# Two layers of a hybrid encoder: four old states to a tile, products of half and quarter width issued side by side

## The chip, the cores and the metric

The kernel runs on one core of one Trainium2 chip. The metric is the device time of one execution in microseconds (us), from the first to the last instruction of the core. PE is the tensor engine (PEld its weight loads), DVE the vector engine, ACT the scalar engine, POOL the GpSimd engine, SP the queue that issues every transfer of this kernel.

## What is computed

A prompt of 256 positions and 8 samples of 16 positions (384 columns in all) pass two layers of width 1024 that share all weights. Each layer has three mixers side by side (windowed attention, a state-space scan, a gated mixing of positions), their projections and gates, and a squared-ReLU block of width 4096. Cut to the two mixers that the change touches:

```python
def sink_attend(q, k, v, valid, sinks):          # 8 query heads in 2 groups of 4, one k/v head a group
    s = jnp.einsum('bcqkgd,bcnkd->bckgqn', q, k) * (HEAD_DIM ** -0.5)
    p = jnp.exp(s - m[..., None])
    o = jnp.einsum('bckgqn,bcnkd->bcqkgd', p, v) / denom

def ssd_scan(x, dt, a, bm, cm, h0):              # h0: old state, 16 heads x 64 x 128 for each sample
    chunk_state = jnp.einsum('bcsgn,bcsgk,bcsgkp->bcgkpn', bc, decay_end, xdt)
    h_new = chunk_decay * h0 + chunk_state       # written out for each sample
    y_inter = jnp.einsum('bctgn,bcgkpn->bctgkp', cc, h_in) * jnp.exp(cum)[..., None]
    y = y_intra + y_inter
```

## The kernel before

**Tiling.** Activations lie with features on the 128 partitions and the 384 columns (256 prompt, 128 samples) along the row. A weight unit is 128 x 1024 f32 (512 KB). SP loads it into one of 4 `raw` tiles (L159), ACT rounds it to a high half (`whi`, L141), DVE subtracts for the low half (`wlo`, L142), 4 tiles of each, and PE multiplies high by high, low by high and high by low, 24 products of 384 columns a unit. These ordinary products fill most of PE's time.

**Order of the work.** The mixers' small products are written as a generator, `chores` (L927): the loops over the weight units call `side()` (L965) before each unit, and a step of the chores is issued there, so that small work lies between ordinary products. A planner then lays the program out over the engines with its own costs; each engine, and SP's queue, runs its instructions in that order. The chores are, layer by layer: turning k and q, `scores` (L651), `turn_p` (L668), `values` (L679) and `attended` (L684) for the prompt, `attn_sample` (L689) for the samples, and `ssd(0)`, `ssd(1)` (L782) for the two groups of state-space heads.

**Scores and values.** The two k/v heads lie on partitions 0 to 63 and 64 to 127. `scores` multiplies all products of one head, then those of the other (64 rows of the array each, into two PSUM banks). `values` writes one head's output to 64 partitions of the bank `po`, so that a product uses 64 columns of the array; it is issued for one head as soon as that head's probabilities are turned, and for the other a step later. For the samples each head has one product of 512 columns and eight of 64.

**Old states.** In `ssd(g)` each of the 8 samples has an old state of 128 x 512 (half the heads). `state` (L895) loads it into a tile of the pool `tm` (12 tiles of 128 x 512). `sample` (L883) multiplies it by 32 columns of `cpad` (L886): C of this sample, with zeros in its neighbour's place, so a product uses 32 columns of the array and all 128 rows, and its 32 partitions of the bank `py` take the sum of two samples. Then PE makes the update from the stacked factors (L890, `stack` and `bm`), POOL scales the old state into a second tile `hn` (L891), DVE adds (L892) and SP writes the result (L893). One sample is one step of the chores:

```python
hn = tm()
mm(py[r, :], cpad[:, b % 2, r], hb, b % 2 == 0, b % 2 == 1)
...
mm(p, bm[:96], d[:96, 0:512], True, True)
pool.tensor_tensor(heads(hn), heads(hb), hb_(decb[:, b, hs]), ALU.mult)
dve.tensor_tensor(hn, hn, p, ALU.add)
```

Beside it run the products within chunks: `decay` (L847, half on POOL, half on DVE, L851) makes the factors of `mask` (L855), and `within` (L864) uses the mask a step later. An f32 product of PE has two records in the trace, a rounded one (`whi`, `wlo`, `stack`, `s1r`) one record.

Of the kernel before, what the change touches and what calls it, by code (L numbers as in the profile page):

```python
# [61 lines left out]
def trunk_kernel(ctx, tc, x_in, c_in, w_ada, sm_in, gf_in, cn_in, wst, wkv, gmc, kc_in, vc_in, hs_in, cs_in,  # L62
# [8 lines left out]
    def nm(s):  # L71
        ids[0] += 1
        return f"{s}{ids[0]}"
# [16 lines left out]
    def mm(out, lhsT, rhs, start, stop):  # L90
        pe.matmul(out, lhsT, rhs, start=start, stop=stop, skip_group_check=True)  # L91
# [53 lines left out]
    class Stream:  # L145
        """The weights of a layer, by group; now and then a part of the modulation's."""
# [66 lines left out]
    def ada(blocks, raws=raw_tile, bank=acc):  # L213
        """Two blocks of the first layer's modulation in three steps: loads, products, the rest."""
# [22 lines left out]
    def ada4(pb):  # L237
        """The rest of the modulation, four blocks at a time; two units of the weights in each step."""
# [41 lines left out]
    class Norm:  # L280
        """1 / sqrt(mean of squares over the features), for each token, in all partitions."""
# [66 lines left out]
    class Early:  # L348
        """The products x * scale, and the shifts beside them: what a layer's first products take while the norm is computed."""
# [24 lines left out]
    def settle(p, rstd, relu):  # L374
        """Products of Early's columns, with the norm and the shifts."""
# [50 lines left out]
    # the tensor engine's clock is up by the time that its first operands are there  # L426
# [31 lines left out]
    def mixers(l, pa, st, h, first):  # L458
        def tm(dt=F32):
            return pa.tile([128, 512], dt, tag="tm", name=nm("tm"), bufs=12)  # L460
# [15 lines left out]
        # gMLP, doubled up to the product  # L476
# [38 lines left out]
        # k, v, dt  # L515
# [12 lines left out]
        # dt = softplus(raw + bias), log1p(e) = 2 atanh(e / (2 + e))  # L528
# [20 lines left out]
        # sums of dt * a: up to t, after s, all; of each sample, all  # L549
# [4 lines left out]
        # q  # L554
# [7 lines left out]
        # rotary  # L562
# [18 lines left out]
        # sums of dt * a: up to t, after s, all; of each sample, all  # L581
# [32 lines left out]
        # gMLP's mixing of positions  # L614
# [53 lines left out]
        def turn_p(i, ng, es, kh):  # L668
            pts = []
            for kt in range(i + 1):  # L670
# [4 lines left out]
                act.copy(pt[:, :ng * 128], p[:, :ng * 128])  # L675
                pts.append(pt)
            return pts
# [6 lines left out]
        def attended(i, g0, ng, po):  # L684
# [4 lines left out]
        def attn_sample():  # L689
# [27 lines left out]
            po = yi()  # L717
            for kh in range(2):
                w = slice(64 * kh, 64 * kh + 64)
                pts = []  # L720
                for src in (pns[kh], pcs[kh]):
# [4 lines left out]
                    act.copy(pt, p)  # L726
# [14 lines left out]
        # convolution  # L741
# [40 lines left out]
        def ssd(g):  # L782
# [35 lines left out]
            # states of the prompt  # L818
# [17 lines left out]
            def stack(j):  # L836
                """The factors of two samples' updates, one below the other: high by high, low by high, high by low."""
# [8 lines left out]
            # within chunks  # L846
# [48 lines left out]
            def state(b):  # L895
                hb = tm()
                sp.dma_start(out=hb, in_=hs_in[l, :, b, half])
                return hb

            todo = [(0, 0), (1, 0), (0, 1), (1, 1), (0, 2), (1, 2)]  # L900
            hb, rs, m, d = state(0), decay(*todo[0]), None, stack(0)
            yield
            for n in range(8):
                if n < 7:
                    nxt = state(n + 1)
                if n % 2 == 0 and n < 6:
                    ahead = stack(n // 2 + 1)
# [7 lines left out]
                sample(n, hb, d)  # L915
                if n % 2:
                    d = ahead
                hb = nxt
                yield
            yin[2] = tm()  # L920
# [6 lines left out]
        def chores():  # L927
# [13 lines left out]
            pts = [turn_p(0, 4, es, kh)for kh in range(2)]  # L941
            turn_q(2)
            yield
            po = yi()
            for kh in range(2):
                values(0, 4, po, kh, pts[kh])
            attended(0, 0, 4, po)
            for g0 in (0, 2):
                es = scores(1, g0, 2, 256)
                yield  # L950
                po = yi()
                pts = turn_p(1, 2, es, 0)
# [275 lines left out]
```

## Time and profile before

| what | value |
|---|---|
| time, median of 3 runs | 1513.43 us (1512.86 to 1515.37) |
| profiled execution, first to last instruction | 1513.4 us |
| PE busy / its weight loads | 1489.4 us (98%) / 1343.3 us |
| DVE, ACT, POOL busy | 918.2, 639.8, 364.7 us |
| old states: loads and writes | 32 and 32 of 256 KB |
| mean DMA rate | 157 GB/s |

The profiled execution is taken over the same stretch as the times, so its span is its own time, and it stands at the median. Busy time is the union of the records of an engine or a group; a matmul's record runs on while the next one starts, so starts are what tells the pace. Times in a timeline are us from the span's start. Layer 0's mixers run from about 60 to 360 us, layer 1's from about 800 to 1100 us; `ssd(0)` and `ssd(1)` of layer 0 have their samples at 222 to 262 and 292 to 340 us.

### The profile page before, as it was taken

To read this page: it belongs to the slowest core of one execution; us is meant where nothing else is said; L and a number is where in the kernel's file an instruction comes from. 1 tells how busy PE (TensorE), PEld (TensorE's weight loads), DVE (VectorE), ACT (ScalarE), POOL (GpSimd) and SP (SyncE) were. 2 spreads that over 40 slices of the span, in tenths; PEclk is the share of its full clock that TensorE was granted. 3 is DMA by queue.
4 is the path that set the end of the run, shared out by engine and by line. 5 is a ranking of instruction groups with operands and counts; after the bars stand their busy time and mean duration, and the time that the engine had idled before them with its cause. 6 is when DMAs were issued, how large, how long until landed. Compare 5 with 4: busy or idle time off the path is not lost.

```text
span 1513.4 us, 22955 instructions
## 1 busy us (share of the span) xinstructions
PE 1489.4 (98%) x8656; PEld 1343.3 (89%) x8656; DVE 918.2 (61%) x1585; ACT 639.8 (42%) x1142; POOL 364.7 (24%) x553
## 2 busy tenths in 40 slices
PE   8999999999999999999999999999999999999997
PEld 6888887879999988889897988878799999999997
DVE  5688856657456855444448887566674667554332
ACT  4466532325335644322225665423253456443221
POOL 3263223340114500011116623233401254000000
PEclk9999999999999999999999999999999999999999
DMA  9453346454344565565552622363533333333331
GB/s 376 155 196 112 116 151 202 165 190 139 140 167 140 172 237 205 210 221 218 213 186 78 213 95 88 116 197 120 181 123 112 126 112 125 126 126 126 126 126 42
DMA packets 79519, 237.04 MB, mean 157 GB/s; under 512 B 10032, under 2 KB 16560, under 8 KB 79408
## 3 DMA queue, kind: packets, MB, share of 16 engines
q1 hardware_dynamic: 79408, 235.57, 44.9%
q8 instruction: 68, 1.11, 0.3%
q14 instruction: 43, 0.35, 0.1%
HBM read 219.21 MB, written 12.39 MB: 153 GB/s over the span
## 4 chain that ended last, share of the span: by engine, by line
PE 95%; DVE 2%; issue 1%; POOL 1%; ACT 1%; DMA 0%; SPq 0%; DVEq 0%; POOLq 0%; ACTq 0%
PE acc L91 74%; PE mx L91 10%; PE yi L91 6%; PE yy L91 4%; PE mx L129 1%; DVE wlo L142 1%; DMA x<-in_x_dram 0%; DVE x L1090 0%; DVE hlo L345 0%; PE yy L129 0%; PE yi L129 0%; ACT whi L141 0%; POOL h L338 0%; PE acc L129 0%; POOL ck L385 0%
## 5 line engine op out<-in xcount | busy, mean ns | idle before, releaser
L142 DVE TENSOR_TENSOR wlo<-raw,whi 128x1024 fp32r<-128x1024 f32 (+1 forms) x296 | 377.6, 1278 | 261.8 <-ACT whi L141 259.0
L141 ACT CAST whi<-raw 128x1024 fp32r<-128x1024 f32 (+1 forms) x296 | 305.5, 1037 | 511.0 <-PE acc L91 422.9
L91 PE MATMUL acc<-hhi,whi 128*128 128x384 f32 x1264 | 433.9, 343 | 3.7 <-ACT ck L1060 2.2
L91 PE MATMUL acc<-hhi,wlo 128*128 128x384 f32 x1264 | 429.0, 339 | 1.0 <-DVE wlo L142 1.0
L91 PE MATMUL acc<-hlo,whi 128*128 128x384 f32 x1264 | 428.6, 341 | 0.0
L91 PEld LDWEIGHTS acc<-hhi,whi 128*128 128x128 f32 x1264 | 237.3, 188 | 30.1 <-ACT ck L1060 11.7
L91 PEld LDWEIGHTS acc<-hlo,whi 128*128 128x128 f32 x1264 | 237.4, 188 | 9.5 <-issue 8.4
L91 PEld LDWEIGHTS acc<-hhi,wlo 128*128 128x128 f32 x1264 | 237.5, 188 | 6.7 <-issue 4.5
L91 PE MATMUL acc<-fhi,whi 128*128 128x384 f32 x512 | 173.8, 339 | 0.0
L91 PE MATMUL acc<-fhi,wlo 128*128 128x384 f32 x512 | 172.0, 336 | 0.0
L91 PE MATMUL acc<-flo,whi 128*128 128x384 f32 x512 | 172.0, 336 | 0.0
L91 PE MATMUL acc<-quad,whi 128*128 128x384 f32 (+1 forms) x576 | 152.6, 343 | 0.0
L91 PEld LDWEIGHTS acc<-quad,whi 128*128 128x128 f32 x576 | 104.7, 188 | 5.4 <-issue 4.9
L91 PEld LDWEIGHTS acc<-fhi,whi 128*128 128x128 f32 x512 | 96.2, 188 | 12.6 <-issue 11.7
L91 PE MATMUL acc<-quad,wlo 128*128 128x384 f32 (+1 forms) x288 | 97.6, 339 | 0.0
L91 PEld LDWEIGHTS acc<-flo,whi 128*128 128x128 f32 x512 | 96.3, 188 | 0.0
L91 PEld LDWEIGHTS acc<-fhi,wlo 128*128 128x128 f32 x512 | 96.2, 188 | 0.0
L367 POOL TENSOR_TENSOR rs<-x,gains 128x128 f32<-128x128 f32 x24 | 28.2, 1177 | 209.2 <-DVE x L419 209.2
L292 POOL TENSOR_TENSOR ck<-x 128x128 f32<-128x128 f32 x5 | 4.9, 982 | 259.4 <-DVE x L419 252.0
L208 ACT CAST fhi<-ck 128x384 fp32r<-128x384 f32 x64 | 32.4, 512 | 52.9 <-DVE ck L1061 52.9
L91 PEld LDWEIGHTS acc<-quad,wlo 128*128 128x128 f32 x288 | 54.3, 189 | 0.2
L768 DVE SCALAR_TENSOR_TENSOR tm<-tm,cwh,tm 128x408 f32<-128x408 f32 x72 | 47.2, 663 | 4.2 <-ACT tm L766 3.8
(338 smaller groups left out, 2115.8 us busy)
## 6 DMA issues: line engine op xcount, KB each, us to landing
raw<-in_wst_dram SPq DMA_DIRECT2D x288, 512.0 KB, 3.3
raw<-in_w_ada_dram SPq DMA_DIRECT2D x52, 512.0 KB, 4.0
early<-in_w_ada_dram SPq DMA_DIRECT2D x44, 512.0 KB, 5.1
tm<-in_hs_dram SPq DMA_DIRECT2D x32, 256.0 KB, 3.3
out_ss_dram<-tm SPq DMA_DIRECT2D x32, 256.0 KB, 2.6
stack<-tm SPq DMA_DIRECT2D x48, 64.0 KB, 2.5
tm<-in_gmc_dram SPq DMA_DIRECT2D x10, 256.0 KB, 4.3
raw<-in_wkv_dram SPq DMA_DIRECT2D x8, 272.0 KB, 2.6
```

Source lines behind the costliest of these rows:

```text
L91: pe.matmul(out, lhsT, rhs, start=start, stop=stop, skip_group_check=True)
L129: pe.transpose(out, in_, ident[:rows, :rows])
L141: act.copy(hi[:, :n], raw[:, :n])
L142: dve.tensor_tensor(lo[:, :n], raw[:, :n], hi[:, :n].bitcast(F32), ALU.subtract)
L208: act.copy(hi, t)
L292: pool.tensor_tensor(t[:, NP:], ap[:, NP:], ap[:, NP:], ALU.mult)
L367: pool.tensor_tensor(smp(s[:, 0:128]), smp(x[:, k, NP:]), bt(a[:, 1:9]), ALU.mult)
L768: dve.scalar_tensor_tensor(y[:, n], xp[:, i:i + 408], cw[:, c, i:i + 1], y[:, n], ALU.mult, ALU.add)
```

## The change

- **Old states:** `states(q)` loads four samples (those with b % 2 == q) in one transfer of 1 MB into a tile `st` of 128 x 4 x 512, two such tiles. `carried(q, st)` issues the four products with `cpad` one behind the other, each on its own 32 columns of the array and its own 32 partitions of `py`. POOL scales and DVE adds in place in `st`, and the result is written from there. The updates from the stacked factors come one step later than before; two stacks are made at the start.
- **Attention:** `scores` takes the two heads in turn; `attended` issues the values of both heads together, as does `attn_sample`; `together` ties them by a dependency without a semaphore to the last copy of turned probabilities, so that the planner places none before it.
- **Pools:** `tm` has 11 tiles instead of 12, and the scratch space kept for descriptors is set to 2048 bytes.

```diff
+    def together(ins, other):
+        tc.add_manual_dep(
+            ins.ins, other.ins.name, mybir.DependencyInfo(mybir.DependencyClass.NoSync, mybir.DependencyReason.DATA), reason="together")
...
-            return pa.tile([128, 512], dt, tag="tm", name=nm("tm"), bufs=12)
+            return pa.tile([128, 512], dt, tag="tm", name=nm("tm"), bufs=11)
...
-            for kh in range(2):
-                r = slice(64 * kh, 64 * kh + 64)
-                for g in range(ng):
+            for g in range(ng):
+                for kh in range(2):
+                    r = slice(64 * kh, 64 * kh + 64)
                     mm(pk[kh][:, g], qT[r, g0 + g, cols[i]], kT[r, 0:nk], True, True)
...
-        def values(i, ng, po, kh, pts):
-            for kt, pt in enumerate(pts):
-                mm(po[64 * kh:64 * kh + 64, :ng * 128], kv[:, kt, 128 + 64 * kh:192 + 64 * kh], pt[:, :ng * 128],
-                   kt == 0, kt == i)
...
+        def attended(i, g0, ng, turned):
+            po = yi()
+            for kt in range(i + 1):
+                for kh in range(2):
+                    m = mm(po[64 * kh:64 * kh + 64, :ng * 128], kv[:, kt, 128 + 64 * kh:192 + 64 * kh],
+                           turned[kh][0][kt][:, :ng * 128], kt == 0, kt == i)
+                    together(m, turned[1][1])
...
-                mm(po[w, :], kv[:, 2, 128 + 64 * kh:192 + 64 * kh], pts[0], True, False)
-                for b in range(8):
-                    c = slice(b * 64, (b + 1) * 64)
-                    mm(po[w, c], vc[:, b, w], pts[1][:, c], False, True)
+            for kh, w in enumerate(halves):
+                together(mm(po[w, :], kv[:, 2, 128 + 64 * kh:192 + 64 * kh], pts[2 * kh], True, False), last)
+            for b in range(8):
+                c = slice(b * 64, (b + 1) * 64)
+                for kh, w in enumerate(halves):
+                    together(mm(po[w, c], vc[:, b, w], pts[2 * kh + 1][:, c], False, True), last)
...
+            def carried(q, st):
+                for j in range(4):
+                    r = slice(32 * j, 32 * j + 32)
+                    mm(py[r, :], cpad[:, q, r], st[:, j], q == 0, q == 1)
+
             def sample(b, hb, d):
-                r = slice(32 * (b // 2), 32 * (b // 2) + 32)
-                hn = tm()
-                mm(py[r, :], cpad[:, b % 2, r], hb, b % 2 == 0, b % 2 == 1)
...
-                pool.tensor_tensor(heads(hn), heads(hb), hb_(decb[:, b, hs]), ALU.mult)
-                dve.tensor_tensor(hn, hn, p, ALU.add)
-                sp.dma_start(out=ss_out[l, :, b, half], in_=hn)
...
+                pool.tensor_tensor(heads(hb), heads(hb), hb_(decb[:, b, hs]), ALU.mult)
+                dve.tensor_tensor(hb, hb, p, ALU.add)
+                sp.dma_start(out=ss_out[l, :, b, half], in_=hb)
+
+            def states(q):
+                st = pa.tile([128, 4, 512], F32, tag="st", name=nm("st"), bufs=2)
+                sp.dma_start(out=st, in_=hs_in[l].rearrange("p (j q) n -> p q j n", q=2)[:, q, :, half])
+                return st
...
-            hb, rs, m, d = state(0), decay(*todo[0]), None, stack(0)
+            sts, rs, m, ds = [states(q) for q in range(2)], decay(*todo[0]), None, [stack(0), stack(1)]
...
+                if n < 2:
+                    carried(n, sts[n])
...
-                sample(n, hb, d)
...
+                if n:
+                    b = n - 1
+                    sample(b, sts[b % 2][:, b // 2], ds[0])
...
+            sample(7, sts[1][:, 3], ds[0])
```

**How the rows move.** A row is an instruction, out<-in with the numbers of the tiles (`x4`: four alike in a row), behind the line of its file. The first place is PE at the first old states of layer 0's `ssd(0)` (`yi` is the bank of `py`, `acc<-quad` and `acc<-hhi` are ordinary products). Before:

```order
L91 MATMUL acc_2570<-quad_1092,whi_2552 128x384
L91 MATMUL acc_2570<-quad_1091,wlo_2553 128x384
L91 MATMUL yi_2322<-tm_2323,cpad 32x512
L91 MATMUL acc_2570<-quad_1091,whi_2552 128x384
L91 MATMUL acc_2570<-quad_1092,whi_2552 128x384
L91 MATMUL acc_2570<-quad_1091,wlo_2553 128x384
L91 MATMUL acc_2610<-hhi_138,whi_2613 128x384
L91 MATMUL acc_2610<-hlo_139,whi_2613 128x384
L91 MATMUL acc_2610<-hhi_138,wlo_2614 128x384
L91 MATMUL mx_2399<-stack_2329,bm_2397 128x512
L91 MATMUL yi_2322<-tm_2375,cpad 32x512
```

and in the changed program:

```order
L91 MATMUL acc_2371<-quad_1092,whi_2353 128x384
L91 MATMUL acc_2371<-quad_1091,wlo_2354 128x384
L91 MATMUL yi_2322<-st_2323,cpad 32x512 x4
L91 MATMUL acc_2400<-raw_2347,sc 32x256 x4
L91 MATMUL mx_2315<-tm_2271,xs_1518 128x512
L91 MATMUL acc_2400<-raw_2348,sc 32x256 x4
L91 MATMUL acc_2399<-hhi_138,whi_2413 128x384
L91 MATMUL acc_2399<-hlo_139,whi_2413 128x384
```

Each old state's product stood alone between ordinary ones, eight times in a group of heads; now four stand together, twice. The next four follow after 24 ordinary products.

The second place is PE at the values of layer 0's second 128 positions, first two heads of each group (`yi<-tm,kv`; `mx<-kT` are scores, `mx<-cn,tm` transposes). Before:

```order
L91 MATMUL acc_1696<-hhi_152,whi_1699 128x384
L91 MATMUL yi_1521<-tm_1525,kv_867 64x256
L91 MATMUL yi_1521<-tm_1530,kv_867 64x256
L129 MATMUL mx_1597<-cn,tm_1456 128x128 x2
L91 MATMUL mx_1658<-kT_1090,wide_1088 128x256 x2
L91 MATMUL acc_1696<-hlo_153,whi_1699 128x384
L91 MATMUL acc_1696<-hhi_152,wlo_1700 128x384
```

and in the changed program, where the products of the other head have joined:

```order
L91 MATMUL acc_1753<-hhi_144,wlo_1757 128x384
L91 MATMUL acc_1753<-hhi_146,whi_1756 128x384
L91 MATMUL yi_1651<-tm_1524,kv_867 64x256
L91 MATMUL yi_1651<-tm_1592,kv_867 64x256
L91 MATMUL yi_1651<-tm_1529,kv_867 64x256
L91 MATMUL yi_1651<-tm_1597,kv_867 64x256
L91 MATMUL mx_1659<-kT_1090,wide_1088 128x256 x2
L91 MATMUL acc_1753<-hlo_147,whi_1756 128x384
```

Before, two products of one head ran here and those of the other head stood alone 13 and 17 rows further on; now the four of both heads are adjacent, heads in turn.

The third place is POOL at the same `ssd(0)`: scalings of the old states (`ex` is their factor), the half of `decay` that POOL makes (`tm<-cn,dtr`), the filling of `cpad`. Before:

```order
L826 TENSOR_TENSOR tm_2272<-tm_2271,ex_1087 128x512
L851 TENSOR_TENSOR tm_2325<-cn,dtr_897 128x512
L851 TENSOR_TENSOR tm_2391<-cn,dtr_897 128x512
L891 TENSOR_TENSOR tm_2395<-tm_2323,ex_1087 128x512
L851 TENSOR_TENSOR tm_2463<-cn,dtr_897 128x512
L891 TENSOR_TENSOR tm_2467<-tm_2375,ex_1087 128x512
L851 TENSOR_TENSOR tm_2537<-cn,dtr_897 128x512
L891 TENSOR_TENSOR tm_2541<-tm_2448,ex_1087 128x512
L891 TENSOR_TENSOR tm_2601<-tm_2514,ex_1087 128x512
```

and in the changed program:

```order
L834 TENSOR_TENSOR tm_2272<-tm_2271,ex_1087 128x512
L901 TENSOR_TENSOR st_2323<-st_2323,ex_1087 128x512 x4
L803 COPY cpad<-xs_1969 128x4x16
L859 TENSOR_TENSOR tm_2327<-cn,dtr_897 128x512
L901 TENSOR_TENSOR st_2325<-st_2325,ex_1087 128x512 x4
L803 COPY cpad<-xs_1969 128x4x16
L859 TENSOR_TENSOR tm_2395<-cn,dtr_897 128x512
L859 TENSOR_TENSOR tm_2460<-cn,dtr_897 128x512
```

The four scalings of a tile now stand together, ahead of the factors that the next masks need.

## Rows read from the trace of the kernel before

**Rows 1.** The page's first part: busy time of each engine and its share.
```profile
PE 1489.4 (98%) x8656; PEld 1343.3 (89%) x8656; DVE 918.2 (61%) x1585; ACT 639.8 (42%) x1142; POOL 364.7 (24%) x553
```

**Rows 2.** The page's chain of work that ended last, by engine.
```profile
PE 95%; DVE 2%; issue 1%; POOL 1%; ACT 1%; DMA 0%; SPq 0%; DVEq 0%; POOLq 0%; ACTq 0%
```

**Rows 3.** Windows: stretch, us, busy per engine, clock, DMA share, GB/s.
```profile
222.00:262.00 40.00, 40.00 (x215) 28.69 (x214) 26.57 (x41) 10.95 (x16) 16.07 (x14) 1.00 0.60 202
```

**Rows 4.** Waits of PE: who, on whom, us in total, times, longest.
```profile
PE mx L91 <- DMA early<-in_w_ada_dram: 3.7, 1, 3.7
```

**Rows 5.** Timeline of PE: start us, us, line, out<-in, shape, records merged.
```profile
108.08 0.33 PE L91 MATMUL acc<-hhi,whi 128*128 128x384 f32 x1
...
110.35 0.34 PE L91 MATMUL acc<-hlo,whi 128*128 128x384 f32 x1
```

**Rows 6.** The same view about a lone product of an old state.
```profile
223.20 0.34 PE L91 MATMUL acc<-quad,wlo 128*128 128x384 f32 x1
223.47 1.04 PE L91 MATMUL yi<-tm,cpad 128*32 128x512 f32 x2
224.44 0.62 PE L91 MATMUL acc<-quad,whi 128*128 128x384 f32 x2
224.90 0.34 PE L91 MATMUL acc<-quad,wlo 128*128 128x384 f32 x1
```

**Rows 7.** The same view about four adjacent products of the modulation.
```profile
542.06 0.34 PE L91 MATMUL acc<-hhi,wlo 128*128 128x384 f32 x1
542.33 0.62 PE L91 MATMUL yy<-raw,sc 128*32 128x512 f32 x2
542.34 0.62 PE L91 MATMUL yy<-early,sc 128*32 128x512 f32 x2
...
543.33 0.44 PE L91 MATMUL acc<-hhi,whi 128*128 128x384 f32 x1
543.61 0.34 PE L91 MATMUL acc<-hlo,whi 128*128 128x384 f32 x1
```

**Rows 8.** Groups by form on PE: count | busy us, mean ns | idle before.
```profile
L91 PE MATMUL yi<-tm,cpad 128*32 128x512 f32 x64 | 33.5, 605 | 0.0
...
L91 PE MATMUL yi<-tm,kv 128*64 128x256 f32 x32 | 10.1, 403 | 0.1
...
L91 PE MATMUL yi<-tm,kv 128*64 128x512 f32 x16 | 8.6, 618 | 0.4 <-ACT tm L675 0.4
...
L91 PE MATMUL yi<-tm,wide 128*64 128x64 f32 x64 | 4.6, 225 | 0.0
```

**Rows 9.** Timeline of PE: the scores of the first 128 positions, layer 0.
```profile
110.62 1.71 PE L91 MATMUL mx<-kT,wide 64*128 64x128 f32 x16
```

**Rows 10.** Groups by form on POOL, 200 to 345 us.
```profile
L891 POOL TENSOR_TENSOR tm<-tm,ex 128x512 f32<-128x512 f32 x16 | 20.1, 1261 | 20.6 <-DMA tm<-in_hs_dram 9.7 <-PE mx L91 6.3 <-DMA stack<-btr 3.4
L851 POOL TENSOR_TENSOR tm<-cn,dtr 128x512 fp32r<-128x512 f32 x12 | 15.8, 1324 | 19.7 <-PE mx L91 9.8 <-DMA out_ss_dram<-tm 5.8 <-DVE tm L209 4.2
```

**Rows 11.** Windows of the projection of q, layer 0, columns as in rows 3.
```profile
66.00:68.00 2.00, 2.00 (x10) 1.62 (x9) 2.00 (x5) 1.87 (x5) 0.28 (x1) 1.00 1.07 414
```

**Rows 12.** Timeline of SP, DVE and PE: a weight's load, its split, its use.
```profile
65.19 0.33 SPq L159 DMA_DIRECT2D raw<-in_wst_dram  x1
...
75.70 1.19 DVE L142 TENSOR_TENSOR wlo<-raw,whi 128x1024 fp32r<-128x1024 f32 x1
...
79.50 0.39 PE L91 MATMUL mx<-wlo,hhi 128*128 128x512 f32 x1
```

**Rows 13.** Waits of SP, 222 to 340 us, the longest in total.
```profile
SPq L159 <- DVE wlo L142: 23.1, 9, 6.5
```

**Rows 14.** The page's DMA issues: count, KB, median us to landing.
```profile
raw<-in_wst_dram SPq DMA_DIRECT2D x288, 512.0 KB, 3.3
...
tm<-in_hs_dram SPq DMA_DIRECT2D x32, 256.0 KB, 3.3
out_ss_dram<-tm SPq DMA_DIRECT2D x32, 256.0 KB, 2.6
```

More of the change, by code (lines that the diff above doesn't have):

```diff
@@ L90, in mm @@
     def mm(out, lhsT, rhs, start, stop):
-        pe.matmul(out, lhsT, rhs, start=start, stop=stop, skip_group_check=True)
+        return pe.matmul(out, lhsT, rhs, start=start, stop=stop, skip_group_check=True)
+    def together(ins, other):
+        tc.add_manual_dep(
+            ins.ins, other.ins.name, mybir.DependencyInfo(mybir.DependencyClass.NoSync, mybir.DependencyReason.DATA), reason="together")
     def one(shape, name):
@@ L674, in turn_p @@
                 pt = tm()
-                act.copy(pt[:, :ng * 128], p[:, :ng * 128])
+                last = act.copy(pt[:, :ng * 128], p[:, :ng * 128])
                 pts.append(pt)
-            return pts
-        def values(i, ng, po, kh, pts):
-            for kt, pt in enumerate(pts):
-                mm(po[64 * kh:64 * kh + 64, :ng * 128], kv[:, kt, 128 + 64 * kh:192 + 64 * kh], pt[:, :ng * 128],
-                   kt == 0, kt == i)
-        def attended(i, g0, ng, po):
+            return pts, last
+        def attended(i, g0, ng, turned):
[5 more added lines that the diff above has]
+                    together(m, turned[1][1])
             pv = po[:, :ng * 128].rearrange("p (g t) -> p g t", g=ng)
@@ L716, in attn_sample @@
                 yield
-            po = yi()
+            pts = []
             for kh in range(2):
-                w = slice(64 * kh, 64 * kh + 64)
-                pts = []
                 for src in (pns[kh], pcs[kh]):
@@ L725, in attn_sample @@
                     pt = tm()
-                    act.copy(pt, p)
+                    last = act.copy(pt, p)
                     pts.append(pt)
                 yield
-                mm(po[w, :], kv[:, 2, 128 + 64 * kh:192 + 64 * kh], pts[0], True, False)
-                for b in range(8):
-                    c = slice(b * 64, (b + 1) * 64)
-                    mm(po[w, c], vc[:, b, w], pts[1][:, c], False, True)
+            po = yi()
+            halves = [slice(64 * kh, 64 * kh + 64) for kh in range(2)]
+            for kh, w in enumerate(halves):
[4 more added lines that the diff above has]
+                    together(mm(po[w, c], vc[:, b, w], pts[2 * kh + 1][:, c], False, True), last)
             pv = po.rearrange("p (b g q) -> p g b q", b=8, g=4)
@@ L890, in sample @@
                 mm(p, bm[:96], d[:96, 0:512], True, True)
-                pool.tensor_tensor(heads(hn), heads(hb), hb_(decb[:, b, hs]), ALU.mult)
-                dve.tensor_tensor(hn, hn, p, ALU.add)
-                sp.dma_start(out=ss_out[l, :, b, half], in_=hn)
[L895 to L898, printed above, removed]
+                pool.tensor_tensor(heads(hb), heads(hb), hb_(decb[:, b, hs]), ALU.mult)
[5 more added lines that the diff above has]
+                return st
             todo = [(0, 0), (1, 0), (0, 1), (1, 1), (0, 2), (1, 2)]
-            hb, rs, m, d = state(0), decay(*todo[0]), None, stack(0)
+            sts, rs, m, ds = [states(q) for q in range(2)], decay(*todo[0]), None, [stack(0), stack(1)]
             yield
             for n in range(8):
[L904 to L907, printed above, removed]
+                j, q = n // 2, n % 2
                 if m is not None:
@@ L914, in ssd @@
                         rs = decay(*todo[n + 1])
-                sample(n, hb, d)
-                if n % 2:
-                    d = ahead
-                hb = nxt
+                if n:
+                    b = n - 1
+                    sample(b, sts[b % 2][:, b // 2], ds[0])
+                    if b % 2:
+                        ds.pop(0)
+                        if b // 2 < 2:
+                            ds.append(stack(b // 2 + 2))
                 yield
+            sample(7, sts[1][:, 3], ds[0])
             yin[2] = tm()
@@ L940, in chores @@
             yield
-            pts = [turn_p(0, 4, es, kh)for kh in range(2)]
+            turned = [turn_p(0, 4, es, kh) for kh in range(2)]
             turn_q(2)
             yield
[L944 to L947, printed above, removed]
+            attended(0, 0, 4, turned)
             for g0 in (0, 2):
@@ L950, in chores @@
                 yield
-                po = yi()
-                pts = turn_p(1, 2, es, 0)
+                turned = [turn_p(1, 2, es, 0)]
                 yield
-                values(1, 2, po, 0, pts)
-                pts = turn_p(1, 2, es, 1)
+                turned.append(turn_p(1, 2, es, 1))
                 yield
-                values(1, 2, po, 1, pts)
-                attended(1, g0, 2, po)
+                attended(1, g0, 2, turned)
             yield from attn_sample()
@@ L1082, in trunk_kernel @@
             if l:
-                h0, first = entry(l, norm, 0, early, lambda: pa.tile([128, 512], F32, tag="tm", name=nm("tm"), bufs=12), "gu")
+                h0, first = entry(l, norm, 0, early, lambda: pa.tile([128, 512], F32, tag="tm", name=nm("tm"), bufs=11), "gu")
             norm, early = mixers(l, pa, streams[l], h0, first)
```

2 lines of the change are left out of this document (1 added, 1 removed).

## The prediction

> **What bounds the kernel.** I read the page's first part, then the chain, then the windows of the stages that the change touches, then PE's waits, and last PE's timeline, start by start. PE is busy 98% of the span [rows 1] and makes 95% of the chain that ended last [rows 2]. In the first stage of the old states, 222 to 262 us, PE has no free moment, at a granted clock of 1.00 (the 2.4 GHz level), while DVE works 26.6 of 40 us, ACT 11.0 and POOL 16.1, and the transfers use 0.60 of the DMA engines [rows 3]. PE's longest wait of the whole execution is 3.7 us, at the start of the program, on a weight [rows 4]. So in the mixers time is what PE's own instructions take, and an instruction's price is read from starts, since a record runs on under the next one. Ordinary products start every (110.35 - 108.08) / 13 = 0.175 us [rows 5]; 0.2% of the time, 3 us, is about what a measurement of this kernel can tell from no change.
>
> **Old states: the main term.** A lone product of an old state stands between starts at 223.20 and 224.90; three ordinary products (223.20 and the two of 224.44) lie in that stretch, so it costs 1.70 - 3 x 0.175 = 1.17 us [rows 6]. There are 32 (64 records [rows 8], two for an f32 product): 37.4 us. Four adjacent products on four column groups, with the same shape of 128 rows, 32 columns of weights and 512 moving columns, exist in the kernel already, in the modulation: from 542.06 to 543.61, less two ordinary products, 1.55 - 0.35 = 1.20 us for all four [rows 7]. They start within hundredths of a microsecond of each other and the next instruction starts as if there had been one. The order of the changed program has seven such fours, and one in layer 1 that a product of another kind cuts into three and one: 7 x 1.20 + 1.20 + 1.17 = 10.8 us. The change takes off **26.6 us** here. The bounds: nothing, if four slices of one tile do not stream together as the two tiles of the modulation do, and some 28, where a four lies next to the modulation's own products of the same shape. I take the row of the same shape.
>
> The Trainium skill ("TensorE: Matmul & The Clock Gate", Part 3 on packing small matmuls) gives less than the number of tiles: 2.38 times for three column tiles and 3.07 times for four row tiles at 512 columns. By 3.07 a four would cost 4 x 1.17 / 3.07 = 1.52 us, an estimate from that page, and the time below would be some 2.5 us higher; the trace's own four give 4 x 1.17 / 1.20 = 3.9 and decide.
>
> **Values of both heads.** A product on 64 columns of the array can have the other head's beside it on the other 64. For the second 128 positions there are 16 products of 256 columns, 10.1 us busy, 0.63 us each [rows 8]. In the new order two of four places have all four products adjacent (two steps in place of four), and two places have three adjacent and one apart (three steps): 16 products in 10 steps, 6 x 0.63 = **3.8 us**. The products of 512 columns are 8 and took 8.6 us, 1.08 each [rows 8]. Those of the first 128 positions (4) stand as before, scores between the heads, and bring nothing. Those of the samples (4) become two pairs: 2 x 1.08 = **2.1 us**. The samples' 32 products of 64 columns took 4.6 us [rows 8], in four strings of eight of one head; now heads alternate: between nothing (if so short a product is bound by its issue) and half. I take half, **2.3 us**, as the fours of rows 7 start hundredths apart.
>
> **Scores.** The first 128 positions' scores alternate between the two halves of the rows now; 8 products took 1.71 us in layer 0 [rows 9] and as many run in layer 1. No row shows whether two row halves run side by side; the bounds are nothing and half, 1.7 us for both layers. I take **1.2**, since the first and last records do not shrink. The scores of 256 columns nearly all stand in pairs of one head as before, so 0.
>
> **What is added or moved.**
> - POOL now makes four scalings in a row, then its half of the factors that the next mask needs: 4 x 1.26 + 1.32 = 6.4 us [rows 10], from the end of the four products, which PE must release. Behind them on POOL is the copy into `cpad`, small. In the new order 33 ordinary products, the second four and four rows of smaller products lie on PE between the first four and that mask: at least 33 x 0.175 + 1.2 = 7.0 us. It is covered, and the cost is 0; if the cover fails it is a rival, below.
> - `ssd(0)`'s states are now asked for in 2 MB before the second weight of the projection of q. At the 414 GB/s that a window there reaches [rows 11] 2.1 MB take 5.1 us. That weight was issued at 65.19, is about 3.3 us under way [rows 14], and its split ended at 76.9, 2.6 us ahead of its use at 79.50 [rows 12]. So it waits in its buffer for some 7 us and the delay of 5.1 is mostly covered, though the weights behind it need not all be so early. Bounds: 0 and 5.1; I take **1.5**. In layer 1 the loads stand a few weights earlier in the order, with the same bounds; I count it into the same 1.5.
> - `ssd(1)`'s loads wait in SP's queue until the results of `ssd(0)` have left their tile, 2.6 us after each is issued [rows 14], and weights stand behind them. In 222 to 340 us SP's weight loads waited 23.1 us for a split to empty a buffer [rows 13]: loads are as far ahead as the buffers let them be, so a few us cost nothing. In the new order PE comes to these states 148 rows after `ssd(0)`'s last update but one, some 25 us at 0.175.
> - 24 transfers fewer on SP: 0, as SP is waiting anyway. Scaling in place, the update a step later: the same instructions, 0. The tie to the last copy can make PE wait for ACT; that wait was 0.4 us in all before [rows 8], 0. One tile fewer in `tm`: the states leave two tiles (loaded state and result) free in their stage, 0 there; at the start of the mixers a step may wait for a tile, which I leave to the range.
>
> **Sum.** 26.6 + 3.8 + 2.1 + 2.3 + 1.2 = 36.0 off, 1.5 on. The profiled execution's span is 1513.4 us, its own time, and it stands at the median of the runs (1513.43). 1513.4 - 36.0 + 1.5 = **1478 us**. With the unknown small terms at their ends (short products and scores 3.5 less, the 2 MB 4 more; or the extra cost nil, modulation neighbours 1.5 and fewer lone entries to the array some 3 more) this case spans 1471 to 1485.
>
> **Rivals.**
> 1. *POOL becomes the wait.* PE, faster now, reaches the masks before POOL has left the scalings. For it: 7.0 us of cover against 6.4 of work is little, and POOL's work is often held until PE or a transfer releases it [rows 10]. Against it: POOL is busy 16 of 40 us there [rows 3], and the smaller products add to the cover. One scaling's time at each of eight fours is 8 x 1.26 = 10 us: 1488. Chance 0.16, 1485 to 1497.
> 2. *The four do not run side by side*, since all stream from one tile: no gain on the states, 1478 + 26.6 = 1505. Against it: the two products from `raw` in rows 7 stream from one tile and overlap. Chance 0.05.
> 3. *Weights come late, and the kernel is slower.* Each `ssd` asks for 2 MB in one piece, with SP's queue behind it. By the rate of rows 11 that is 5.1 us; at eight landings of 256 KB one after the other, 8 x 3.3 = 26 us [rows 14]. From 36 / 4 = 9 us of uncovered delay at each of the four, the gain is gone; at 12 the time is 1513.4 - 36 + 48 = 1525. Against it: the waits of rows 13 show several buffers of lead, and only one of the four loads stands where the lead is short [rows 12]. Chance 0.03.
>
> That the change does not do what it says is in part so, and already in the sum: the order leaves the first positions' values and most wide scores unpaired.
>
> **Numbers.** Forecast 0.74; POOL 0.16; not side by side 0.05; late weights 0.03; below 1471, 0.02. The range 1471 to 1490 holds the forecast and the nearer part of the first rival, some 0.82. Faster by over 0.2% are all but the third rival, whose nearer half is within 0.2%: 0.96, 0.02, 0.02.
>
> **What would show it.** Group of the old states' products: busy near 9 x 1.04 = 9.4 us [rows 6] in place of 33.5. Values of 256 columns near 6.3 us, of 64 near 2.3. PE still without waits between 222 and 340 us; a mask or a `stack` product that waits for POOL means rival 1, a wait on `wlo` between 75 and 100 us means that the 2 MB were felt. DVE, ACT and POOL busy as before. I am wrong if the old states' group keeps more than 15 us, or if PE's waits grow by more than 6 us.

## The result, and the profile after the change

The changed kernel takes 1479.39 us (median of 4 runs, 1477.70 to 1480.29) against 1514.40 us for the kernel before beside it (1512.86 to 1515.56): a ratio of 0.9766, with a 95% interval of 0.9753 to 0.9779. That is 35 us, 2.3%, faster; the prediction said 1478, between 1471 and 1490. The experiments below are compared by such ratios; 0.001 is 1.5 us. A run's time is not the span of its profile: in every run that lists both, the time is 1.7 to 2.3 us longer (here 1479.59 against 1477.4), so the 1513.4 us of the profile before belong to a time some 2 us above, and not to the median. Spans are compared with spans below, times with times.

The page of the profiled execution after the change, first its head and PE's busy time [rows 1], then the chain that ended last [rows 2]:

```profile
span 1477.4 us, 22859 instructions
...
PE 1453.0 (98%) x8656; PEld 1337.2 (91%) x8656; DVE 917.5 (62%) x1585; ACT 639.7 (43%) x1142; POOL 377.3 (26%) x553
...
PE 90%; DVE 3%; DMA 2%; POOL 2%; issue 1%; ACT 1%; SPq 0%; DVEq 0%; POOLq 0%; ACTq 0%
```

PE's busy time fell from 1489.4 to 1453.0 us, by 36.4, and the span from 1513.4 to 1477.4, by 36.0. PE stood idle for 24.0 us before and for 24.4 after. So the whole gain is work that PE no longer does one product after the other, and almost nothing of it was given back as a wait. The chain has more of DMA (2%) and POOL (2%) in it than before. POOL's busy time rose by 12.6 us, which the prediction did not expect: 5.0 of it are the scalings (38.0 to 43.0 us, a mean of 1193 and 1373 ns each); where the rest comes from I have not followed.

Where the work went is in the groups by form of the changed kernel: count | busy us, mean ns of a record | idle before, and who ended it.

```profile
L91 PE MATMUL mx<-stack,bm 96*128 96x512 f32 x32 | 12.6, 403 | 0.0
...
L91 PE MATMUL yi<-st,cpad 128*32 128x512 f32 x64 | 9.6, 605 | 0.0
L91 PE MATMUL mx<-kT,wide 64*128 64x256 f32 x32 | 8.6, 405 | 0.0
...
L91 PE MATMUL yi<-tm,kv 128*64 128x512 f32 x16 | 6.4, 618 | 0.9 <-ACT tm L680 0.9
L91 PE MATMUL yi<-tm,kv 128*64 128x256 f32 x32 | 5.6, 395 | 0.0
...
L91 PE MATMUL mx<-kT,wide 64*128 64x128 f32 x32 | 2.3, 285 | 0.0
L91 PE MATMUL yi<-tm,wide 128*64 128x64 f32 x64 | 2.2, 222 | 0.0
```

Counts and the mean of a record are those of [rows 8]: a record still takes some 605 ns. Only the busy time is smaller, 9.6 in place of 33.5 us for the old states, since records now lie on top of each other. The values went from 10.1 to 5.6 (256 columns), from 8.6 to 6.4 (512) and from 4.6 to 2.2 us (64).

PE's timeline in layer 1, start us and us, shows one four between ordinary products; x8 are the records of four products:

```profile
1016.70 0.33 PE L91 MATMUL acc<-quad,wlo 128*128 128x384 f32 x1
1016.96 1.06 PE L91 MATMUL yi<-st,cpad 128*32 128x512 f32 x8
1017.96 0.44 PE L91 MATMUL acc<-hhi,whi 128*128 128x384 f32 x1
1018.23 0.34 PE L91 MATMUL acc<-hlo,whi 128*128 128x384 f32 x1
```

From 1016.70 to 1018.23 are 1.53 us, with two ordinary products of 0.175 in them: 1.18 us for four old states, where one alone took 1.17 [rows 6]. Another part of the timeline, layer 0's scores [rows 9] and the samples' values of both heads:

```profile
108.99 1.16 PE L91 MATMUL mx<-kT,wide 64*128 64x128 f32 x16
...
189.84 1.08 PE L91 MATMUL yi<-tm,kv 128*64 128x512 f32 x4
190.75 1.10 PE L91 MATMUL yi<-tm,wide 128*64 128x64 f32 x32
```

The scores took 1.71 us before and take 1.16 now, so products on the two halves of the rows do overlap. Two products of 512 columns take 1.08 us for both heads, what one took alone, and sixteen products of 64 columns take 1.10.

The stage of the first old states, which begins now at 200 us, by windows (start:end, length, busy us of PE, PEld, DVE, ACT and POOL with counts, granted clock, DMA share, GB/s) [rows 3]:

```profile
200.00:240.00 40.00, 40.00 (x259) 33.23 (x257) 32.15 (x47) 14.07 (x20) 20.57 (x17) 1.00 0.54 181
```

PE is still never idle and its clock stays at 1.00; 259 records lie in these 40 us, where the window of before held 215. DVE went from 26.57 to 32.15 us and POOL from 16.07 to 20.57. The two windows do not hold exactly the same work; DVE's busy time in the whole execution is the same as before (917.5 and 918.2 us).

### The profile page after: what moved, and what is told of

It is laid out like the page before. It is cut to its first block, busy times and chain, and to the rows that moved or that the text cites. A ratio compares the mean times of both kernels' runs of the same rounds, so it can differ in the third digit from the quotient of the medians.

```text
span 1477.4 us, 22859 instructions
## 1 busy us (share of the span) xinstructions
PE 1453.0 (98%) x8656; PEld 1337.2 (91%) x8656; DVE 917.5 (62%) x1585; ACT 639.7 (43%) x1142; POOL 377.3 (26%) x553
## 4 chain that ended last, share of the span: by engine, by line
PE 90%; DVE 3%; DMA 2%; POOL 2%; issue 1%; ACT 1%; SPq 0%; DVEq 0%; POOLq 0%; ACTq 0%
PE acc L91 73%; PE mx L91 8%; PE yy L91 4%; PE yi L91 3%; PE mx L134 1%; DVE wlo L147 1%; POOL st L901 1%; DMA st<-in_hs_dram 1%; DMA early<-in_w_ada_dram 1%; DMA x<-in_x_dram 0%; POOL tm L859 0%; ACT L513 0%; DVE x L1097 0%; DVE hlo L350 0%; DMA stack<-tm 0%
## 5 line engine op out<-in xcount | busy, mean ns | idle before, releaser
L91 PEld LDWEIGHTS acc<-hhi,whi 128*128 128x128 f32 x1264 | 237.3, 188 | 24.9 <-ACT ck L1067 12.6
L91 PEld LDWEIGHTS acc<-fhi,whi 128*128 128x128 f32 x512 | 96.2, 188 | 12.6 <-issue 11.7
```

The source lines that it names most:

```text
L91: return pe.matmul(out, lhsT, rhs, start=start, stop=stop, skip_group_check=True)
```

## The experiments

The theory: PE's own time is the bound, and the change makes column groups and row halves run side by side, so the time falls by what PE saves. Rivals: the gain comes from fewer transfers and updates in place; it comes from adjacency alone; POOL or the 2 MB loads eat a part of it. Eleven kernels ran, each of them in five rounds beside the kernel before; one was the changed kernel itself, which came out at 0.9767 (0.9753 to 0.9780):

> The changed kernel once more, on the chip of the next runs, so that they are compared with it directly: 0.975 to 0.978 of the kernel before.

### One part at a time

`e1_states` has the old states' part with the attention of before; `e2_attention` has attention's part with the old states of before. Cut to the core, against the changed kernel:

```diff
 e1_states
-            for kt in range(i + 1):
-                for kh in range(2):
-                    m = mm(po[64 * kh:64 * kh + 64, :ng * 128], ...
-                    together(m, turned[1][1])
+        def values(i, ng, po, kh, pts):
+            for kt, pt in enumerate(pts):
+                mm(po[64 * kh:64 * kh + 64, :ng * 128], ...
 e2_attention
-                if n < 2:
-                    carried(n, sts[n])
+                mm(py[r, :], cpad[:, b % 2, r], hb, b % 2 == 0, b % 2 == 1)
```

> Only the old states' part of the change; attention as in the kernel before. Theory (PE's own time is the bound, so what a part takes off PE comes off the time): 26.6 us off for the fours, up to 1.5 on for the 2 MB loads: 1487 to 1488.5 us, group of the old states' products near 9.6 us busy. Rival (the two parts work only together, or the gain of the whole came from attention): within 3 us of the kernel before.

> Only attention's part; old states one at a time, as in the kernel before. Theory: PE's groups after the whole change shrank by 4.5 (256 columns), 2.2 (512), 2.4 (64), 1.1 and 0.7 (scores), 10.9 us together, and the prediction had 9.4; the time falls by 9 to 11 us, to 1502.5 to 1504.5. Rival (the shorter products are covered or given back as waits for the turned halves): less than 5 us.

Measured: the states alone 0.9834 of the kernel before (0.9819 to 0.9848), 25.2 us off; attention alone 0.9927 (0.9912 to 0.9941), 11.1 us off. Together 36.3, where the whole change took 35.4 off by its ratio: the parts add up. PE's busy time, 1489.4 us before, is 1467.3 and 1477.0 us in the two, 22.1 and 12.4 less; each is within 3.1 us of what the ratio says, and an interval here is some 2 us wide on either side. In the first kernel the group of the old states has 10.4 us, 0.8 more than expected, as its order cuts two of the fours into one and three (the changed kernel's cuts one). 25.2 lies at the lower edge of what was expected.

### What makes the four cheap

Three kernels keep the changed kernel's loads, its tile and its updates in place, and alter only how the products of the old states stand.

```diff
 e3_one_per_step
-                if n < 2:
-                    carried(n, sts[n])
+                carried(q, sts[q], j)
 e9_two
+                if n < 4:
+                    carried(q, sts[q], (2 * j, 2 * j + 1))
 e7_one_group
-                    mm(py[r, :], cpad[:, q, r], st[:, j], q == 0, q == 1)
+                    mm(py[0:32, :] if q else py[r, :], cpad[:, q, r], st[:, j], q == 0, j == 3 if q else j > 0)
```

> The changed kernel, with its one load of four states, its updates in place and its attention, but one old state's product in each step in place of four at once. Theory (the gain is the adjacency on PE): 32 lone products of 1.17 us are back in place of 10.8 us, so 26.6 us more than the changed kernel, about 1505; a few us less where the order leaves two of them side by side; group back near 33 us busy. Rival (the gain is that of fewer transfers, fewer tiles and updates in place): within 4 us of the changed kernel, 1476 to 1483.

> The changed kernel with the old states' products in twos (two column groups, a step apart) in place of fours. Theory (a step costs what its 512 columns cost and its way in and out, however many column groups run): 15 twos and 2 singles, 17 x 1.17 to 1.20 = 20 us in place of 10.8, so 9 to 10 us slower than the changed kernel, group near 17 to 18 us busy. Rival (each product beyond the first has a price of its own): nearer to the changed kernel, 4 to 7 us slower.

> The changed kernel, with the second four of each half on the first column group: still four adjacent products from one tile, same shapes, but all onto the same 32 columns of weights and the same 32 rows of the result, so the samples' parts of the old states' product are summed wrongly into one group. Theory (the gain is that four column groups run side by side): the four changed fours cost 4 x 0.9 to 1.17 us each in place of 1.20, so 10 to 14 us slower than the changed kernel. Rival (adjacency alone, one way in and out of the shape, is the gain): within 3 us of it.

Measured: one per step 0.9944 (0.9930 to 0.9959), 27 us slower than the changed kernel; twos 0.9825 (0.9811 to 0.9838), 9 us slower; four on one column group 0.9832 (0.9818 to 0.9845), 10 us slower. The groups of the three, in this order:

```profile
L91 PE MATMUL yi<-st,cpad 128*32 128x512 f32 x64 | 33.5, 605 | 0.0
```

```profile
L91 PE MATMUL yi<-st,cpad 128*32 128x512 f32 x64 | 17.9, 605 | 0.0
```

```profile
L91 PE MATMUL yi<-st,cpad 128*32 128x512 f32 x64 | 20.0, 600 | 0.0
```

The first is the group of before to the tenth of a microsecond [rows 8]. By time it is 8.5 us faster than the kernel before, and `e2_attention`, which has the old loads and updates, was 11.1 us faster beside the same runs: one load of four states, 24 transfers fewer, updates in place and the smaller pool bring no gain by themselves, and may cost some 2 us. The last tells adjacency and column groups apart; its timeline at a four on one group:

```profile
957.42 0.34 PE L91 MATMUL acc<-hhi,wlo 128*128 128x384 f32 x1
957.69 3.62 PE L91 MATMUL yi<-st,cpad 128*32 128x512 f32 x8
961.24 0.44 PE L91 MATMUL acc<-hhi,whi 128*128 128x384 f32 x1
961.52 0.34 PE L91 MATMUL acc<-hlo,whi 128*128 128x384 f32 x1
```

957.42 to 961.52, less two ordinary products, are 3.75 us for four adjacent products that share a column group. A two of `e9_two` on two groups between ordinary products:

```profile
222.28 0.34 PE L91 MATMUL acc<-quad,wlo 128*128 128x384 f32 x1
222.55 1.05 PE L91 MATMUL yi<-st,cpad 128*32 128x512 f32 x4
223.53 0.44 PE L91 MATMUL acc<-hhi,whi 128*128 128x384 f32 x1
223.82 0.34 PE L91 MATMUL acc<-hlo,whi 128*128 128x384 f32 x1
```

1.54 - 0.35 = 1.19 us. So a string between ordinary products costs (3.75 - 1.18) / 3 = 0.86 us for each product on its busiest column group, and 1.18 - 0.86 = 0.32 us for the way in and out of the shape, and it does not matter how many of the four groups run: one product, two and four cost 1.17, 1.19 and 1.18 us. The rival of adjacency alone has fallen: it would have left `e7_one_group` where the changed kernel is. Columns of the array and rows of the result go together in this run, so it does not tell which of the two makes the four wait for each other.

### The 2 MB ahead of the weights

`e4_loads_later` ties the loads of `states` to the weight last asked for, which puts those of `ssd(0)` 32 transfers later in layer 0.

```diff
+            self.asked = sp.dma_start(out=r[:, :U], in_=wst[self.l, GROUPS[group][0] + n])
...
+                load = sp.dma_start(out=t, in_=hs_in[l].rearrange("p (j q) n -> p q j n", q=2)[:, q, :, half])
+                together(load, st.asked)
```

> The changed kernel, with the 2 MB loads of the first half's states asked for 32 transfers later in layer 0, and as many in layer 1, behind the weights that the projection of q needs. Theory of the prediction (the 2 MB delay those weights and cost 1.5 us, at most 5.1): 0.5 to 2 us faster than the changed kernel, 1477.5 to 1479. Rival (the weights' lead covered all): the same within 0.7 us. A third way: the states then come late to their first four, and it is slower by what PE waits for them.

Measured: 0.9763 (0.9748 to 0.9778), the same as the changed kernel. The time alone does not choose between the two forecasts: they lie 0.5 to 2 us apart, and the interval is some 2 us wide on either side. What chooses is where PE waits. In the changed kernel the weight behind the 2 MB goes like this (SP, DVE and PE; as in [rows 12]):

```profile
64.44 0.83 SPq L164 DMA_DIRECT2D raw<-in_wst_dram  x1
...
77.42 1.22 DVE L147 TENSOR_TENSOR wlo<-raw,whi 128x1024 fp32r<-128x1024 f32 x1
...
81.69 0.73 PE L91 MATMUL mx<-wlo,hhi 128*128 128x512 f32 x2
```

It is asked for 0.75 us earlier than before, is 10.7 us under way where it was 4.8, and is split 1.72 us later, so the loads were felt by the transfer. They were not felt by PE: the first use came at 81.69 in place of 79.50, since the new order sets other products ahead of it. The old use, moved up by the same 0.75 us, would have come at 78.75, and the split ended at 78.64: this weight would have been in time, by 0.1 us, in the old order too. PE's waits between 60 and 102 us, of the kernel before, of the changed kernel, and of the one with later loads:

```profile
PE acc L91 <- DVE wlo L142: 0.8, 1, 0.8
PE mx L91 <- ACT tm L560: 0.7, 2, 0.5
```

```profile
PE mx L91 <- ACT tm L565: 0.6, 1, 0.6
PE mx L91 <- POOL tm L765: 0.2, 1, 0.2
```

```profile
PE acc L91 <- DVE wlo L147: 1.0, 1, 1.0
PE mx L91 <- ACT tm L565: 0.5, 1, 0.5
```

The `wlo` wait that the prediction named as the mark of a felt load is not there with the early loads; it is there before the change, and where the loads come later. So the loads cost PE nothing that its waits show. The order of PE differs between the two, so what this does not show is the price of the loads at an order that is held.

### How much cover POOL has

`e8_pool_twice` doubles the suspected work, a multiplication by 1 behind each scaling:

```diff
                 pool.tensor_tensor(heads(hb), heads(hb), hb_(decb[:, b, hs]), ALU.mult)
+                pool.tensor_tensor(heads(hb), heads(hb), hb_(ones[:, 0:8]), ALU.mult)
```

> The changed kernel, with each of the 32 scalings followed on POOL by a multiplication by 1 of the same size: 32 x 1.0 to 1.26 us more work on POOL, 32 to 40 us, in the place where the prediction saw 6.4 us of work under 7.0 us of cover. If that cover were all, each of the eight fours would stall PE for some 3.5 to 4.5 us, 28 to 36 us in all (about 1510). Theory after the traces seen so far (PE hardly waits for POOL even with eight scalings in a row, so the cover is much longer): within 4 us of the changed kernel, with waits of PE for POOL under 2 us more.

Measured: 0.9849 (0.9836 to 0.9863), 12 us slower than the changed kernel, so neither bound was right. PE's waits in this kernel (us in total, times, longest), and the windows about the wait at 307 us:

```profile
PE mx L91 <- POOL tm L859: 7.3, 4, 3.1
```

```profile
304.00:306.00 2.00, 2.00 (x17) 1.75 (x17) 1.39 (x1) 0.00 (x0) 2.00 (x2) 1.00 0.41 110
306.00:308.00 2.00, 0.99 (x12) 0.62 (x6) 0.98 (x3) 0.62 (x1) 2.00 (x3) 1.00 0.35 82
308.00:310.00 2.00, 0.22 (x1) 0.22 (x2) 0.83 (x2) 0.00 (x0) 2.00 (x3) 0.82 0.48 188
310.00:312.00 2.00, 2.00 (x6) 1.61 (x7) 0.54 (x1) 0.60 (x1) 0.72 (x1) 0.50 0.00 0
312.00:314.00 2.00, 2.00 (x8) 2.00 (x7) 1.74 (x5) 0.47 (x1) 0.00 (x0) 0.50 0.16 41
314.00:316.00 2.00, 2.00 (x8) 2.00 (x7) 1.23 (x1) 0.97 (x2) 0.00 (x0) 0.50 0.53 179
316.00:318.00 2.00, 2.00 (x13) 2.00 (x12) 0.55 (x1) 0.00 (x0) 0.34 (x1) 0.98 0.54 181
```

Waits are 7.3 us, and the changed kernel has 0.2 on that line. Much of the rest is the clock: after PE had waited 2.8 us here, it was granted 0.50, the 1.2 GHz level, from 310 to 316 us, and did in these 6 us the work of 3. The same happened after the wait of 3.1 us near 1058; a wait of 1.2 us at 225 left the clock at 1.00. Two times some 3 us, the waits of 7.3, and 1 us for a four that this order cuts give 14, against 12 to 13 by the ratios and 15.6 between the spans of the two profiled executions. The sum is rough: PE's idle time as a whole rose by only 5.3 us (24.4 to 29.7), as other waits got shorter, and a third stretch at 0.50, from 101.0 to 104.5 us, cost some 1.7 us more. That one came behind waits of 0.6 and 0.2 us, which the changed kernel has at the same place at a clock of 1.00; what brought it on is open.

So rival 1 of the prediction is a real mechanism and near: the changed kernel has 4.1 to 6.2 us of scalings behind each four and is 0.2 us short of cover at one place, in layer 1; with twice the work there are four waits at eight fours. POOL at that place in the changed kernel, and then PE's wait on it:

```profile
1018.67 5.93 POOL L901 TENSOR_TENSOR st<-st,ex 128x512 f32<-128x512 f32 x4
1024.57 2.02 POOL L859 TENSOR_TENSOR tm<-cn,dtr 128x512 fp32r<-128x512 f32 x1
1026.55 5.14 POOL L901 TENSOR_TENSOR st<-st,ex 128x512 f32<-128x512 f32 x4
1031.65 2.02 POOL L859 TENSOR_TENSOR tm<-cn,dtr 128x512 fp32r<-128x512 f32 x1
```

```profile
PE mx L91 <- POOL tm L859: 0.2, 1, 0.2
```

POOL works here for 15 us without a break. The second four's products begin at 1022.83, but its scalings only at 1026.55, behind the work of the first four. What PE's products have to cover is thus the work of both fours together, where the prediction weighed that of one.

### Without the ties

`e10_no_ties` makes `together` do nothing.

> The changed kernel without the ties to the last copy; the code still asks for both halves together. In the order the samples' 512-column pairs fall apart (2 places, 1.0 us each) and two places of 256 columns have three steps in place of two (0.6 us each); the 64-column pairs stay. Theory: 2 to 3.3 us slower than the changed kernel by PE's groups, less up to 1 us of waits for a copy that go away. Rival: the ties do all of attention's gain, and it is 9 to 11 us slower.

Measured: 0.9812 (0.9799 to 0.9825), 7 us slower than the changed kernel; I had expected 2 to 3.3. Its groups:

```profile
L91 PE MATMUL yi<-st,cpad 128*32 128x512 f32 x64 | 11.6, 605 | 0.0
...
L91 PE MATMUL yi<-tm,kv 128*64 128x512 f32 x16 | 8.6, 618 | 0.9 <-ACT tm L679 0.9
...
L91 PE MATMUL yi<-tm,kv 128*64 128x256 f32 x32 | 6.9, 398 | 0.0
L91 PE MATMUL yi<-tm,wide 128*64 128x64 f32 x64 | 2.9, 226 | 0.0
```

Against the changed kernel that is 2.0 + 2.2 + 1.3 + 0.7 = 6.2 us. The values' groups of 256 and 512 columns make 3.5 of it, a little more than the upper end of the expectation. The expectation missed two things: not all of the 64-column pairs stayed, and the order that comes out without the ties also cuts two more fours of the old states, work that the ties do not touch. Nor did the wait for the copy go away.

### More pairs

`e5_pairs` issues the half that comes last first, ties the other products to it, and ties the wide scores to the last copy. `e6_eight` has this too, and both fours of a half in one step.

```diff
 e5_pairs
-            for kt in range(i + 1):
-                for kh in range(2):
+            lead = turned[1][1]
+            for kt in reversed(range(i + 1)):
+                for kh in (1, 0):
...
-                    together(m, turned[1][1])
+                    together(m, lead)
+                    if kh and kt == i:
+                        lead = m
 e6_eight
-                if n < 2:
-                    carried(n, sts[n])
+                if not n:
+                    for k in range(2):
+                        carried(k, sts[k])
```

> The changed kernel with the rest of the pairs: the values' products of the first 128 positions are issued last half first, so that the order puts both halves beside each other (2 places, 2 x 1.08 us), all four places of 256 columns have their four adjacent (2 steps of 0.63 us fewer), and the wide scores wait for the same copy. Theory: 2 to 4 us faster than the changed kernel, group of 512 columns near 4.3 us busy in place of 6.4, of 256 near 5.0 in place of 5.6. Rival (one of the pair waits for its copy and PE with it): no gain.

> The run before, with both fours of each half in one step, eight adjacent products. Theory: a four's 1.20 us is mostly its 512 columns, and the way in and out of it some 0.15 to 0.3 us; joined four times this saves 0.6 to 1.2 us, which one measurement can hardly tell; all eight scalings stand earlier on POOL, 8 x 1.26 us in a row, and if POOL's cover fails the time is up to 10 us longer. Rival: more than 4 us faster, which would say that the edges cost more than the products.

Measured, on the chip of the changed kernel's second measurement (0.9767): pairs 0.9769 (0.9756 to 0.9783), no gain; eight 0.9746 (0.9733 to 0.9760), 1477.5 us against 1480.7. The groups of `e6_eight`:

```profile
L91 PE MATMUL yi<-st,cpad 128*32 128x512 f32 x64 | 8.7, 600 | 0.0
L91 PE MATMUL mx<-kT,wide 64*128 64x256 f32 x32 | 8.2, 408 | 0.9 <-ACT tm L682 0.9
...
L91 PE MATMUL yi<-tm,kv 128*64 128x256 f32 x32 | 4.3, 392 | 0.0
L91 PE MATMUL yi<-tm,kv 128*64 128x512 f32 x16 | 4.3, 618 | 0.0
```

The values' groups are what was expected, in `e5_pairs` too: 2.1 and 1.3 us less than the changed kernel. Yet PE's busy time fell by only 1.6 us there (1453.4 to 1451.8), and the stretch from the start of the first score to the end of the last value by 0.8 to 0.9 us in each layer (82.9 to 82.0 and 82.6 to 81.8). Neighbours' groups rose by some tenths each, as the modulation's products on 256 columns from 14.2 to 14.6; I have not followed all of it. 1.6 us is less than this measurement tells from nothing. The eights' group is 0.9 us shorter again, and a string of eight in layer 1 took 2.04 us, as 0.32 + 2 x 0.86 would have it. PE waited for no mask although eight scalings stand in a row on POOL. `e6_eight` is the fastest kernel of the study, by 3 us, but its interval overlaps that of the changed kernel, and the profiles account for 1.6 + 0.9 = 2.5 of them.

## Why the prediction was right

- **Old states, 26.6 us.** The price of a four from the modulation's row [rows 7] was right: 1.18 to 1.20 us between ordinary products, 0.80 where a four lies next to the modulation's products (the four at 201.80). All of them together cost 10.3 us by starts, where the sum had 10.8. The states alone brought 25.2 us, with one four more cut. The Trainium skill ("TensorE: Matmul & The Clock Gate", Part 3) gives 3.07 times for four row tiles, and its table has no row for four column tiles alone; the runs give 4 x 1.17 / 1.18 = 4.0 for four column tiles, so here the trace decides.
- **Values.** 3.8 predicted and 4.5 measured at 256 columns; 2.1 and 2.2 at 512; 2.3 and 2.4 at 64. For the last the prediction took the upper of its bounds, nothing and half, and half it is: sixteen products of both heads now take 1.10 us, about what eight of one head took. At 256 the price of a step was too high for steps that follow each other: ten steps now take 5.6 us, 0.56 each and not 0.63, since most of them stand two in a string and share its way in and out.
- **Scores.** 1.2 predicted, 1.1 measured. The wide scores fell from 9.3 to 8.6 us where the sum had 0: at one place of layer 1 the order does alternate the halves in part.
- **Not in the sum.** The samples' updates (`mx<-stack,bm`) fell from 13.9 to 12.6 us, although nothing was done to them. Before, 10 of the 32 stood right behind a lone product of an old state, and their records took 0.50 us, those behind most other products 0.40; now none stands there. Part of this may already be in the 1.17 us of a lone product.
- **The 2 MB, +1.5.** This is the term that was wrong. No wait of PE shows it, and the weight wait of 0.8 us that the kernel before had in that stretch was gone. That the transfer would be late was right, by 5.9 us against an estimate of 5.1. The prediction also took PE's order there as given, when the changed order uses that weight 2.2 us later; but the old use, moved up with the rest, would still have found it split, so whether the new order was needed to hide the loads is not shown.
- **POOL, 0.** Right in size, though the 0.6 us to spare were not there at one place, where PE waits 0.2 us: there the work of two fours stood in a row. Its price as a rival was put at one scaling for each four; that left out the clock, which in `e8_pool_twice` cost some 3 us more behind each of the two waits of 2.8 and 3.1 us.

So the mechanism was right, and the near hit of the number is in part luck. 36.0 off and 1.5 on 1513.4 make 1478.9, which the prediction wrote as 1478. It started from a span and was held against a time, and a time is some 2 us longer: by spans 1477.4 was measured, 1.5 below the sum, by the median 1479.4, 0.5 above it. The change itself was put at 34.5 us; it is 36.0 by the spans and 35.0 by the medians. PE saved 36.4 us by its busy time, and 0.4 came back as idle time. The terms measured above, 27.1 (37.4 - 10.3) + 4.5 + 2.2 + 2.4 + 1.1 + 0.7, make 38.0, so 1.6 us of what the groups gained is not found in the whole; groups overlap at their edges, and which others rose was not followed. Each of these differences is smaller than the spread of the runs.

## What to carry to other kernels

In this kernel a string of narrow products cost what its busiest column group cost, plus one way in and out of the shape. So look for lone narrow products, price them by starts and not by records, and find in the same kernel a place where the tiles already run side by side: it gives the price of the change before it is made. Then read the order that comes out, and not the code that asks for it, since both a tie elsewhere and a higher row can cut a string in two. When PE is at 98%, look at what stands behind the products that it now does sooner: here one place was 0.2 us short of the time that POOL needed.

## What the runs showed of the hardware that was not expected

Products of 64 rows on the two halves of the rows overlapped, 1.16 us for eight in place of 1.71, and products on the two halves of the columns ran side by side even with only 64 moving columns: the samples' 16 such products took 1.10 us, 0.14 us for a pair of heads. Two adjacent column groups cost the same as four, 1.19 and 1.18 us. And the two waits of 2.8 and 3.1 us for POOL in `e8_pool_twice` were each followed by some 6 us of work at a granted clock of 0.50. The changed kernel itself has such a place: a wait of 3.1 us on a weight's split ends near 798 us, and from 798 to 800 the granted clock is 0.52.
